# A two-layer hybrid decoder trunk on one core: one residue for the weight buffers, another order of the first loads, and small work moved off VectorE

## The chip, the cores and the metric

One core of one Trainium2 chip runs the whole program. The metric is the device time of one execution in microseconds. Three runs of the kernel before took 906.34, 906.39 and 908.03 us, median 906.39. Engines are named as the profile names them: PE is TensorE's matmul, PEld its weight load, DVE is VectorE, ACT is ScalarE, POOL is GpSimd, SP is SyncE, which issues most transfers.

## What is computed

Two layers act on x (256 tokens, 1,024 features, float32), conditioned by one vector c:

```python
c_act = silu(c)
for l in range(2):
    shift, scale, gate = split(c_act @ ada_w[l] + ada_b[l], 3)      # adaLN
    h = rmsnorm(x, norm_g[l]) * (1 + scale) + shift
    a_x, a_g, b_q, b_k, b_v, b_g, c_q, c_k, c_v, c_g, m_g = split(h @ w_in[l])
    ya = rg_lru(causal_conv4(a_x), ...) * silu(a_g)                 # softplus(lambda) sets the decay
    yb = merged_dilated_attention(rope(qknorm(b_q)), rope(qknorm(b_k)), b_v) * silu(b_g)
    yc = rmsnorm(gla(c_q, c_k, c_v, decay(h))) * silu(c_g)
    mg = sigmoid(m_g)                                               # three gates of 1024
    merged = mg[0]*(ya @ proj_a) + mg[1]*(yb @ proj_b) + mg[2]*(yc @ proj_c)
    x = x + gate * (merged @ w_o[l])
```

All of it is float32 to nearly full accuracy.

## The kernel before

**Products.** A float32 product is made of three fp32r matmuls: each operand is split into a rounded part `hi` and a rest `lo`, and hi·hi, hi·lo and lo·hi are summed in PSUM. x and h are kept with features on the partitions: eight tiles of 128 features x 256 tokens (`hhi`, `hlo`).

**Units.** The weights are streamed from HBM as 144 units a layer, each of 1,024 (or 768, 800) words a partition. A "T" unit (q, k, v, bg, c; two of the eight feature tiles) goes through `mm_t` (L777): h is stationary and the weights are the moving operand, 384, 400 or 512 columns; for bg the weights are stationary. An "F" or "P" unit (ax, ag, cq, ck, mA, mB, mC, pA, pB, pC, wo) goes through `mm_f` (L803): the weights are stationary, eight blocks of 128 x 128, and h, the merged input or a branch output (`yhi`, `ylo`) is the moving operand, 256 columns. Each step of a unit is three matmuls (L807 to L809, or L799 to L801). The first group of units of a layer is q, k, v, bg of head pair 0, four times: units 0 to 15.

**Buffers.** `load_next` (L191) issues a unit's transfer into one of six `raw` buffers. `advance` (L211) makes `hi` on ScalarE (L232) and `lo` on VectorE (L233) for the unit three ahead, in one of four `whi` and four `wlo` buffers; then the raw buffer is free and the next transfer is issued. `whi` and `wlo` are 1,040 words a partition, of which a unit takes the words from `o` on, `o` being 0 or 16 by the parity of its number and its kind (L224, L225).

**Where things lie.** Pools are laid out in the order in which they are opened, tiles in the order of their first use, each padded to 32 bytes a partition: `head` (vec_sb, c_sb, pos_sb, 896 bytes), `wts` (six raw, four whi, four wlo), `mov` (h), `one`, `two`, `sml`. By this the raw buffers start at a multiple of 256 bytes, and so do `wts` and `mov` as wholes; the four whi buffers are handed out in the order 0, 3, 2, 1. `yhi` starts 128 bytes past a multiple of 256.

**The start.** SP issues c, eye, x in two halves, vec, and then the items of `stream` (L84): four columns of adaLN (128 x 1024 each), units 0 to 3, four columns, units 4 to 7 and so on until 16 columns and units 0 to 15 are in. silu(c) is spread over the partitions (`crow`, L309 to L324) by eight small matmuls. `ada_tile` (L330) makes one column of shift or scale with a multiply-and-reduce on VectorE (L334), for a scale the product with norm_g (L336), and, once a pair is there, the tile of h (`h_tile`, L363): `tmp` = x · scale · rstd on VectorE (L366), `hi` on ScalarE (L368), `lo` on VectorE (L369). rstd comes from `stats_start` (L377), squares on ScalarE, three additions on VectorE, two matmuls with ones, and `rstd_full` (L346). The splits of units 0 to 3 are ordered behind rstd (`issue_after`, L230, L231).

**Small work.** `tables` (at unit 2) loads positions and makes the rope angles (`angles`, L419, VectorE but for two sines) and `rope_tables` (L441, eight VectorE products). `small` (at unit 16) makes softplus of lambda (`softplus`, L396, on VectorE but for one exponential) for the gates of branch A (`gen_a`, L502: sp4, sp4n, hb). The rest of the work of the branches is cut into generators that `pump` (L759) advances after each unit by a budget. A scheduler orders instructions on each engine's queue by priority and the `issue_after` marks.

```python
        if it in early:
            raw_t[n] = early[it]
            cur["sy", "a", it[2]] = SY.dma_start(out=early[it], in_=ada[it[1], it[2]]).ins
            return load_next()
```

Of the kernel before, what the change touches and what calls it, by code (L numbers as in the profile page):

```python
# [10 lines left out]
F32 = mybir.dt.float32  # L11
F32R = mybir.dt.float32r
# [114 lines left out]
def hybrid_trunk(ctx: ExitStack, tc: tile.TileContext, ws, ada, vec, gates, a2, qkg, c_t, x_t, pos, inv, eye,  # L127
# [13 lines left out]
    wts = ctx.enter_context(tc.tile_pool(name="wts", bufs=LEAD + 1))  # L141
    mov = ctx.enter_context(tc.tile_pool(name="mov", bufs=1))
# [165 lines left out]
    cact = sml.tile([P, KT], F32, name="cact")  # L308
    crow = one.tile([P, KT, P], F32, name="crow")  # L309
# [6 lines left out]
    V.tensor_scalar(b1, b1, 1.0, None, ALU.add)  # L316
    diag = one.tile([P, KT, P], F32, name="diag", tag="pt0")
    V.tensor_tensor(diag, eye_sb.unsqueeze(1).to_broadcast([P, KT, P]), cact.unsqueeze(2).to_broadcast([P, KT, P]), ALU.mult)
# [5 lines left out]
    crow2 = crow.rearrange("p k n -> p (k n)")  # L324

# [4 lines left out]
    def ada_tile(l, c, w):  # L330
# [61 lines left out]
    sp4 = sml.tile([P, L, KT], F32, name="sp4")  # L392
    sp4n = sml.tile([P, L, KT], F32, name="sp4n")
    hb = sml.tile([P, L, 2 * KT], F32, name="hb")

    def softplus():  # L396
        lam = vec_sb[:, :, V_LAM:V_LAM + KT]
        e, s, s2, p = (sml.tile([P, L, KT], F32, name=f"spl{i}") for i in range(4))
        V.scalar_tensor_tensor(e, lam, -1.0, lam, ALU.mult, ALU.max)
        A.activation(e, e, AF.Exp, scale=-1.0)  # L400
        V.tensor_scalar(s, e, 2.0, None, ALU.add)
        V.reciprocal(s, s)
        V.tensor_tensor(s, s, e, ALU.mult)
        V.tensor_tensor(s2, s, s, ALU.mult)
        V.tensor_scalar(p, s2, 1.0 / 17.0, None, ALU.mult)
        for k in range(7, 0, -1):
            V.scalar_tensor_tensor(p, p, 1.0 / (2 * k + 1), s2, ALU.add, ALU.mult)
        V.scalar_tensor_tensor(p, p, 1.0, s, ALU.add, ALU.mult)
        V.tensor_scalar(e, lam, -1.0, 0.0, ALU.mult, ALU.max)
        V.scalar_tensor_tensor(p, p, 2.0, e, ALU.mult, ALU.add)  # L410
        V.tensor_scalar(sp4, p, 0.5 * LRU_C, None, ALU.mult)
        V.tensor_scalar(sp4n, p, -0.5 * LRU_C, None, ALU.mult)
        V.tensor_scalar(hb, vec_sb[:, :, V_BA:V_BA + 2 * KT], 0.5, None, ALU.mult)
# [5 lines left out]
    def angles():  # L419
        pf = sml.tile([P, 2], F32, name="an0")  # L420
        an, k = (two.tile([P, 2, 32], F32, name="an", tag=t) for t in ("ra", "rb"))
        V.tensor_copy(pf, pos_sb)
        for t in range(2):
            V.tensor_scalar(an[:, t], inv_sb, pf[:, t:t + 1], None, ALU.mult)
        V.tensor_scalar(k, an, float(1.0 / (2 * np.pi)), 12582912.0, ALU.mult, ALU.add)
        V.tensor_scalar(k, k, -12582912.0, None, ALU.add)
        c1 = 6.28125
        c2 = float(np.float32(np.round((2 * np.pi - c1) * 2**21) / 2**21))
        c3 = float(2 * np.pi - c1 - c2)
        for c in (c1, c2, c3):  # L430
            V.scalar_tensor_tensor(an, k, -c, an, ALU.mult, ALU.add)
# [9 lines left out]
    def rope_tables(l):  # L441
# [5 lines left out]
        for i in range(2):  # L447
            g = gq[:, i].rearrange("p g (e d) -> p g e d", e=2)
            for t in range(2):
                V.tensor_tensor(ct[:, i, t].rearrange("p g (e d) -> p g e d", e=2), g,  # L450
                                cs[:, t].unsqueeze(1).unsqueeze(1).to_broadcast([P, 3, 2, 32]), ALU.mult)
                V.tensor_tensor(st[:, i, t].rearrange("p g (e d) -> p g e d", e=2), g,
                                sn[:, t].unsqueeze(1).to_broadcast([P, 3, 2, 32]), ALU.mult)
# [520 lines left out]
    def small():  # L974
# [3 lines left out]
        V.tensor_scalar(vec_sb[:, :, V_ON:V_ON + 2], vec_sb[:, :, V_ON:V_ON + 2], 0.5, None, ALU.mult)  # L978
# [102 lines left out]
```

## Time and profile before

| | |
|---|---|
| median of 3 runs | 906.39 us (906.34 to 908.03) |
| the profiled execution | 906.63 us, of which the span of instructions is 904.9 us |
| TensorE busy | 865.6 us, 96% of the span, 6,340 matmuls |
| VectorE busy | 671.9 us, 74% |
| ScalarE busy | 531.8 us, 59% |
| GpSimd busy | 179.1 us, 20% |
| HBM | 168 MB read, 187 GB/s over the span |
| granted TensorE clock | 0.987 of full, over the span |

A stretch's row gives the busy time of each engine with the number of instructions, the granted clock, the share of the 16 DMA engines that was in use and the rate. A timeline row gives the start, the duration, engine, line and operands of one instruction, and in brackets the idle time of its engine before it and what ended that. Matmuls are pipelined: how fast they follow each other is read from their starts.

### The profile page before, as it was taken

The numbers are of one execution on the slowest core, as the hardware profiler recorded it, in microseconds if no ns is written. First come the engines' busy times: TensorE is split into PE (matmuls) and PEld (weight loads), VectorE is DVE, ScalarE is ACT, GpSimd is POOL, SyncE is SP. The second block draws the span as 40 slices with busy tenths as digits, with TensorE's granted clock in tenths as the row PEclk, the third lists the DMA queues.
The fourth block names the chain that finished last, engine by engine and source line by source line (L and its number), as shares of the span: only waits on it lengthen the run. The fifth ranks groups of instructions, "written<-read, shape, count | busy, mean of one in ns | idle before, by whom it ended". The sixth has DMA issues, their size and how long they took to land.

```text
span 904.9 us, 16407 instructions
## 1 busy us (share of the span) xinstructions
PE 865.6 (96%) x6340; PEld 818.7 (90%) x6340; DVE 671.9 (74%) x1115; ACT 531.8 (59%) x897; POOL 179.1 (20%) x160
## 2 busy tenths in 40 slices
PE   3989999999999999999999999989999999999998
PEld 2978999999988888998989999979999988899998
DVE  6998899669667667656776788986896666656674
ACT  4376976686544554644454689666874545554451
POOL 0026365224000110100030525651430001000000
PEclk7999999999999999999999999999999999999999
DMA  8884456446756666676654644553567455455651
GB/s 334 309 290 138 146 174 193 141 134 195 248 184 197 205 212 201 212 236 205 224 168 148 191 146 144 176 194 117 184 205 239 163 189 166 148 173 187 191 167 47
DMA packets 52111, 170.16 MB, mean 188 GB/s; under 512 B 6240, under 2 KB 8160, under 8 KB 52032
## 3 DMA queue, kind: packets, MB, share of 16 engines
q1 hardware_dynamic: 51216, 167.04, 56.8%
q10 hardware_dynamic: 672, 1.87, 0.7%
q8 instruction: 50, 0.82, 0.4%
q0 software_dynamic: 144, 0.20, 0.2%
q14 instruction: 29, 0.24, 0.1%
HBM read 168.23 MB, written 1.05 MB: 187 GB/s over the span
## 4 chain that ended last, share of the span: by engine, by line
PE 51%; DVE 19%; DMA 12%; issue 8%; ACT 5%; POOL 4%; DVEq 0%; SPq 0%; ACTq 0%
DMA raw<-in_ada_dram 10%; PE mm L807 10%; PE mm L809 10%; PE mm L808 10%; DVE wlo L233 8%; PE mm L799 5%; PE mm L800 5%; PE mm L801 4%; POOL ss L570 2%; PE xps L177 1%; ACT whi L232 1%; DVE raw L334 1%; DVE rb L564 1%; DMA g_raw<-in_gates_dram 1%; DVE ra L562 1%
## 5 line engine op out<-in xcount | busy, mean ns | idle before, releaser
L233 DVE TENSOR_TENSOR wlo<-raw,whi 128x1024 fp32r<-128x1024 f32 (+2 forms) x288 | 335.3, 1171 | 84.5 <-ACT whi L232 83.1
L232 ACT CAST whi<-raw 128x1024 fp32r<-128x1024 f32 (+2 forms) x288 | 280.1, 976 | 185.2 <-PE mm L808 120.4
L807 PE MATMUL mm<-hhi,whi 128*128 128x256 f32 x768 | 217.1, 283 | 2.9 <-DVE rb L564 2.9
L809 PE MATMUL mm<-hhi,wlo 128*128 128x256 f32 x768 | 216.0, 282 | 3.5 <-DVE wlo L233 3.5
L808 PE MATMUL mm<-hlo,whi 128*128 128x256 f32 x768 | 215.4, 280 | 0.0
L799 PE MATMUL mm<-whi,hhi 128*128 128x384 f32 (+2 forms) x480 | 169.5, 358 | 7.2 <-ACT hhi L368 6.5
L800 PE MATMUL mm<-wlo,hhi 128*128 128x384 f32 (+2 forms) x480 | 171.3, 358 | 1.6 <-DVE wlo L233 1.4
L801 PE MATMUL mm<-whi,hlo 128*128 128x384 f32 (+2 forms) x480 | 167.6, 355 | 0.5 <-DVE hlo L369 0.5
L807 PEld LDWEIGHTS mm<-hhi,whi 128*128 128x128 f32 x768 | 146.0, 190 | 4.5 <-ACT tmp L857 2.9
L809 PEld LDWEIGHTS mm<-hhi,wlo 128*128 128x128 f32 x768 | 145.6, 190 | 4.7 <-DVE wlo L233 4.1
L808 PEld LDWEIGHTS mm<-hlo,whi 128*128 128x128 f32 x768 | 145.7, 190 | 0.3
L799 PEld LDWEIGHTS mm<-whi,hhi 128*128 128x128 f32 x480 | 92.9, 195 | 14.5 <-ACT hhi L368 7.5
L800 PEld LDWEIGHTS mm<-wlo,hhi 128*128 128x128 f32 x480 | 93.4, 195 | 9.1 <-DVE wlo L233 3.2
L334 DVE CUSTOM_DVE_ANT_0 raw<-raw,crow,vec_sb 128x1024 f32<-128x1024 f32 x38 | 48.7, 1283 | 70.2 <-DMA raw<-in_ada_dram 70.2
L801 PEld LDWEIGHTS mm<-whi,hlo 128*128 128x128 f32 x480 | 92.5, 194 | 6.7 <-DVE hlo L369 0.8
L807 PE MATMUL mm<-yhi,whi 128*128 128x256 f32 x320 | 89.9, 281 | 1.5 <-DVE mg L949 1.5
L808 PE MATMUL mm<-ylo,whi 128*128 128x256 f32 x320 | 89.4, 279 | 0.0
L809 PE MATMUL mm<-yhi,wlo 128*128 128x256 f32 x320 | 89.2, 279 | 0.0
L807 PEld LDWEIGHTS mm<-yhi,whi 128*128 128x128 f32 x320 | 60.4, 189 | 2.5 <-DVE mg L949 1.7
L809 PEld LDWEIGHTS mm<-yhi,wlo 128*128 128x128 f32 x320 | 60.1, 188 | 0.8 <-DVE mod L334 0.4
L808 PEld LDWEIGHTS mm<-ylo,whi 128*128 128x128 f32 x320 | 60.1, 188 | 0.0
L708 POOL TENSOR_TENSOR at_hl<-att_sb,at_hl 128x384 fp32r<-128x384 f32 x8 | 8.8, 1096 | 206.3 <-ACT at_hl L707 206.3
(236 smaller groups left out, 1409.2 us busy)
## 6 DMA issues: line engine op xcount, KB each, us to landing
raw<-in_ws_dram SPq DMA_DIRECT2D x192, 512.0 KB, 4.2
raw<-in_ws_dram SPq DMA_DIRECT2D x88, 384.0 KB, 3.1
raw<-in_ada_dram SPq DMA_DIRECT2D x38, 512.0 KB, 4.5
raw<-in_ws_dram SPq DMA_DIRECT2D x8, 400.0 KB, 4.6
g_raw<-in_gates_dram ACTq DMA_DIRECT2D x3, 512.0 KB, 4.5
x_sb<-in_x_t_dram SPq DMA_DIRECT2D x2, 512.0 KB, 6.6
ada_yhi<-in_ada_dram SPq DMA_DIRECT2D x2, 512.0 KB, 7.8
ada_ylo<-in_ada_dram SPq DMA_DIRECT2D x2, 512.0 KB, 9.0
```

What stands on the lines that cost most here:

```text
L177: seen[0] = T.transpose(*a, **k).ins
L232: A.copy(hi, r)
L233: V.tensor_tensor(lo, r, hi.bitcast(F32), ALU.subtract)
L334: V.tensor_tensor_reduce(w, w, crow2, 1.0, b, ALU.mult, ALU.add, a if i == 0 else m)
L562: V.tensor_tensor(ra.rearrange("p (g s) d -> p g s d", g=3), z4, ctab[l][:, i, t].unsqueeze(2).to_broadcast(bc), ALU.mult)
L570: G.tensor_tensor(ss, ss, mhalf[:, 0:12].rearrange("p (a b) -> p a b", a=2), ALU.pow)
L799: T.matmul(o, ah, wh, start=(k == 0), stop=False)
L800: T.matmul(o, ah, wl, start=False, stop=False)
L801: T.matmul(o, al, wh, start=False, stop=(k == KT - 1))
L807: T.matmul(ps[:, 0:S], hi[:, a:b], xh[:, k], start=(k == 0), stop=False)
L808: T.matmul(ps[:, 0:S], hi[:, a:b], xl[:, k], start=False, stop=False)
L809: T.matmul(ps[:, 0:S], lo[:, a:b], xh[:, k], start=False, stop=(k == nk - 1))
```

## The change

Buffers: `whi` and `wlo` become 1,024 words; `o` is 16 for q, k and v and 0 for all others. `sp4` and `hb` (64 and 128 bytes a partition) move from `sml` to `head`, in front of the weights; `sp4n` (64 bytes) gets a pool of its own, `gap`, between `wts` and `mov`.

Start: adaLN columns 0 and 1 are issued ahead of x, and vec is issued from ScalarE's queue. Matmuls without use (`warm_up`) are added: eight on `ones` before the silu, two on `diag`, three within `rstd_full`. The sum of squares takes eight matmuls and no additions. The tile of h is made otherwise: VectorE multiplies x by rstd, a few tiles at a time and without the scale (`x_scaled`); ScalarE makes scale · xr + shift (`f`), then `hi`; VectorE subtracts. The product with norm_g goes to ScalarE. The order marks of units 0 to 3 change: the rounded parts of units 1 to 3 come after the first rounded tile of h, the rests after the first scaled x. `tables` is no longer ordered behind VectorE's part of the last h.

Small work: softplus but for the reciprocal, and the angles but for one operation, go to GpSimd (a fused pair of operations becomes two there) and ScalarE; the rope tables take two products instead of eight.

```diff
+    gap = ctx.enter_context(tc.tile_pool(name="gap", bufs=1))
...
             cur["sy", "a", it[2]] = SY.dma_start(out=early[it], in_=ada[it[1], it[2]]).ins
+            if it[2] == 1:
+                for i in range(2):
+                    SY.dma_start(out=x_sb[:, 4 * i:4 * i + 4], in_=x_t[:, 4 * i:4 * i + 4])
...
-                streamed = units[it[1]][1][0] == "T" and units[it[1]][1][1] != "bg"
-                o = 16 * ((it[1] % 2 == 0) != streamed)
-                hi = wts.tile([P, D + 16], F32R, name="whi", tag="whi")[:, o:o + e]
-                lo = wts.tile([P, D + 16], F32R, name="wlo", tag="wlo")[:, o:o + e]
+                o = 16 * (units[it[1]][1][1] in ("q", "k", "v"))
+                hi = wts.tile([P, D], F32R, name="whi", tag="whi")[:, o:o + e]
+                lo = wts.tile([P, D], F32R, name="wlo", tag="wlo")[:, o:o + e]
                 with ExitStack() as st:
                     if it[1] < 4:
-                        st.enter_context(tc.issue_after(cur["ra"]))
-                        st.enter_context(tc.issue_after(cur["rv"]))
+                        st.enter_context(tc.issue_after(cur["h0a" if it[1] else "ra"]))
                     A.copy(hi, r)
+                with ExitStack() as st:
+                    if it[1] < 4:
+                        st.enter_context(tc.issue_after(cur["xr0"]))
                     V.tensor_tensor(lo, r, hi.bitcast(F32), ALU.subtract)
...
+    sp4 = head.tile([P, L, KT], F32, name="sp4")
+    hb = head.tile([P, L, 2 * KT], F32, name="hb")
+    sp4n = gap.tile([P, L, KT], F32, name="sp4n")
...
+    A.dma_start(out=vec_sb, in_=vec)
     SY.dma_start(out=eye_sb, in_=eye)
-    for i in range(2):
-        SY.dma_start(out=x_sb[:, 4 * i:4 * i + 4], in_=x_t[:, 4 * i:4 * i + 4])
-    SY.dma_start(out=vec_sb, in_=vec)
...
+    warm_up(ones, 8)
...
+    warm_up(diag[:, 0:2].rearrange("p k n -> p (k n)"), 2)
...
-            V.tensor_tensor(m, a, vcol(l, V_NG + j), ALU.mult)
+            A.activation(m, a, AF.Copy, scale=vcol(l, V_NG + j))
         if l == 0 and i == 1:
-            h_tile(0, j, cur["rstd"], cur["h"])
+            h_first(j, cur["xr"], cur["h"])
...
+    def x_scaled(i, a, b):
+        if a == 0:
+            cur["xr"][i] = one.tile([P, 4, S], F32, name="xr", tag=("pt1", "pt0")[i])
+        v = V.tensor_tensor(cur["xr"][i][:, a:b], x_sb[:, 4 * i + a:4 * i + b],
+                            cur["rstd"].unsqueeze(1).to_broadcast([P, b - a, S]), ALU.mult)
+        cur.setdefault("xr0", v.ins)
+
+    def h_first(j, xr, h):
+        if j in (1, 2, 4):
+            x_scaled(j // 4, j % 4, 2 if j == 1 else 4)
+        hi, lo, f = h[0], h[1], tmp()
+        A.activation(f, xr[j // 4][:, j % 4], AF.Identity, bias=mod[:, 0, 1, j:j + 1], scale=mod[:, 0, 0, j:j + 1])
+        a = A.copy(hi[:, j], f)
+        cur.setdefault("h0a", a.ins)
+        v = V.tensor_tensor(lo[:, j], f, hi[:, j].bitcast(F32), ALU.subtract)
+        cur["h_last"] = (a.ins, v.ins)
...
-            if i % 2:
-                V.tensor_tensor(sq[i - 1], sq[i - 1], t, ALU.add)
-        V.tensor_tensor(sq[0], sq[0], sq[2], ALU.add)
         ps = xps()
-        for j in range(2):
-            T.matmul(ps[:, 0:S], ones, sq[0][:, j], start=(j == 0), stop=(j == 1))
+        for j in range(KT):
+            T.matmul(ps[:, 0:S], ones, sq[j // 2][:, j % 2], start=(j == 0), stop=(j == KT - 1))
...
-        for k in range(7, 0, -1):
-            V.scalar_tensor_tensor(p, p, 1.0 / (2 * k + 1), s2, ALU.add, ALU.mult)
+        for k in range(6, -1, -1):
+            G.tensor_tensor(p, p, s2, ALU.mult)
+            G.tensor_scalar(p, p, 1.0 / (2 * k + 1), None, ALU.add)
...
         for c in (c1, c2, c3):
-            V.scalar_tensor_tensor(an, k, -c, an, ALU.mult, ALU.add)
+            G.tensor_scalar(kc, k, -c, None, ALU.mult)
+            G.tensor_tensor(an, an, kc, ALU.add)
...
-    rstd = rstd_full(sts)
+    rstd = rstd_full(sts, 3)
+    cur["rstd"], cur["xr"] = rstd, {}
+    x_scaled(0, 0, 1)
...
         a, v = cur["h_last"]
-        with tc.issue_after(a), tc.issue_after(v):
+        with tc.issue_after(a):
```

## Rows read from the trace of the kernel before

**Rows 1.** Busy time by stretch, whole program: us, busy us (x instructions) by engine

```profile
20.00:40.00 20.00, 19.66 (x115) 19.65 (x116) 20.00 (x39) 8.23 (x12) 0.00 (x0) 0.88 0.88 327
40.00:60.00 20.00, 18.67 (x115) 16.92 (x114) 19.79 (x45) 10.51 (x16) 2.89 (x1) 1.00 0.93 331
60.00:80.00 20.00, 15.79 (x116) 14.98 (x115) 19.88 (x44) 14.11 (x30) 13.38 (x13) 0.91 0.45 151
80.00:905.00 825.00, 805.95 (x5982) 762.67 (x5980) 599.96 (x960) 490.58 (x827) 161.45 (x141) 1.00 0.56 179
```

**Rows 2.** Transfers by line: size and median us from issue to landing

```profile
x_sb<-in_x_t_dram SPq DMA_DIRECT2D x2, 512.0 KB, 6.6
...
ada_yhi<-in_ada_dram SPq DMA_DIRECT2D x2, 512.0 KB, 7.8
```

**Rows 3.** Timeline of the start: start us, duration us, instruction

```profile
7.95 2.27 ACT L381 ACTIVATE sq<-x_sb 128x512 f32<-128x512 f32 x4 [5.32 <-DMA x_sb<-in_x_t_dram]
...
11.82 2.05 PE L388 MATMUL xps<-sq,ones 128*128 128x256 f32 x4 [3.76 <-DVE sq L385]
...
18.02 0.42 DVE L357 SCALAR_TENSOR_TENSOR rs_y<-rs_q,rs_y 128x256 f32<-128x256 f32 x1
18.36 0.98 DVE L233 TENSOR_TENSOR wlo<-raw,whi 128x800 fp32r<-128x800 f32 x1
...
20.34 0.70 PE L799 MATMUL mm<-whi,hhi 128*128 128x400 f32 x1 [6.47 <-ACT hhi L368]
```

**Rows 4.** Timeline of TensorE, four F units one behind the other

```profile
164.32 0.28 PE L808 MATMUL mm<-hlo,whi 128*128 128x256 f32 x1
...
169.74 0.28 PE L809 MATMUL mm<-hhi,wlo 128*128 128x256 f32 x1
...
175.18 0.28 PE L809 MATMUL mm<-hhi,wlo 128*128 128x256 f32 x1
```

**Rows 5.** Timeline of TensorE, T units of 384 columns

```profile
119.45 0.34 PE L801 MATMUL mm<-whi,hlo 128*128 128x384 f32 x1
...
121.19 0.34 PE L799 MATMUL mm<-whi,hhi 128*128 128x384 f32 x1
...
124.70 0.34 PE L801 MATMUL mm<-whi,hlo 128*128 128x384 f32 x1
```

**Rows 6.** Groups of VectorE and ScalarE by line: busy us, mean ns

```profile
L366 DVE SCALAR_TENSOR_TENSOR tmp<-x_sb,mod,rs_y 128x256 f32<-128x256 f32 x8 | 3.7, 479 | 0.0
L384 DVE TENSOR_TENSOR sq<-sq 128x512 f32<-128x512 f32 x2 | 1.4, 692 | 4.9 <-ACT sq L381 4.9
L336 DVE TENSOR_TENSOR mod<-acc,vec_sb 128x1 f32<-128x1 f32 x8 | 1.2, 153 | 0.0
L431 DVE SCALAR_TENSOR_TENSOR an<-an 128x64 f32<-128x64 f32 x3 | 0.7, 218 | 0.0
...
L407 DVE SCALAR_TENSOR_TENSOR spl<-spl,spl 128x16 f32<-128x16 f32 x7 | 2.0, 284 | 0.0
...
L368 ACT ACTIVATE hhi<-tmp,mod 128x256 fp32r<-128x256 f32 x8 | 4.0, 509 | 10.1 <-DVE tmp L366 10.1
```

**Rows 7.** Timeline of VectorE and GpSimd, small operations

```profile
60.93 0.18 DVE L407 SCALAR_TENSOR_TENSOR spl<-spl,spl 128x16 f32<-128x16 f32 x1
...
62.73 1.66 POOL L568 TENSOR_TENSOR ro<-ra,rb 128x192 f32<-128x192 f32 x1
...
63.87 0.56 DVE L407 SCALAR_TENSOR_TENSOR spl<-spl,spl 128x16 f32<-128x16 f32 x1
...
71.70 0.20 POOL L569 TENSOR_SCALAR ss<-ss 128x12 f32<-128x12 f32 x1
```

**Rows 8.** Busy time by stretch: the granted clock is the third number from the end

```profile
20.30:24.40 4.10, 4.06 (x13) 4.05 (x14) 4.10 (x7) 1.32 (x2) 0.00 (x0) 0.50 1.02 412
...
65.00:70.00 5.00, 2.31 (x18) 2.15 (x17) 5.00 (x11) 3.35 (x9) 1.27 (x3) 0.90 0.86 278
70.00:75.00 5.00, 5.00 (x36) 4.99 (x35) 5.00 (x13) 1.98 (x4) 4.83 (x5) 0.76 0.50 163
```

More of the change, by code (lines that the diff above doesn't have):

```diff
@@ L315, in hybrid_trunk @@
     b1 = vec_sb[:, :, V_ADA:V_ADA + 16].rearrange("p l (j i) -> p l j i", i=2)[:, :, :, 0]
-    V.tensor_scalar(b1, b1, 1.0, None, ALU.add)
     diag = one.tile([P, KT, P], F32, name="diag", tag="pt0")
-    V.tensor_tensor(diag, eye_sb.unsqueeze(1).to_broadcast([P, KT, P]), cact.unsqueeze(2).to_broadcast([P, KT, P]), ALU.mult)
+    v = V.tensor_tensor(diag, eye_sb.unsqueeze(1).to_broadcast([P, KT, P]), cact.unsqueeze(2).to_broadcast([P, KT, P]), ALU.mult)
+    with tc.issue_after(v.ins):
+        V.tensor_scalar(b1, b1, 1.0, None, ALU.add)
     for e in range(2):
@@ L382, in stats_start @@
             sq.append(t)
-            if i % 2:
-                V.tensor_tensor(sq[i - 1], sq[i - 1], t, ALU.add)
-        V.tensor_tensor(sq[0], sq[0], sq[2], ALU.add)
         ps = xps()
-        for j in range(2):
-            T.matmul(ps[:, 0:S], ones, sq[0][:, j], start=(j == 0), stop=(j == 1))
-        return ps
-    sp4 = sml.tile([P, L, KT], F32, name="sp4")
-    sp4n = sml.tile([P, L, KT], F32, name="sp4n")
-    hb = sml.tile([P, L, 2 * KT], F32, name="hb")
+        for j in range(KT):
+            T.matmul(ps[:, 0:S], ones, sq[j // 2][:, j % 2], start=(j == 0), stop=(j == KT - 1))
+        return ps
     def softplus():
@@ L398, in softplus @@
         e, s, s2, p = (sml.tile([P, L, KT], F32, name=f"spl{i}") for i in range(4))
-        V.scalar_tensor_tensor(e, lam, -1.0, lam, ALU.mult, ALU.max)
+        A.activation(e, lam, AF.Abs)
         A.activation(e, e, AF.Exp, scale=-1.0)
-        V.tensor_scalar(s, e, 2.0, None, ALU.add)
+        G.tensor_scalar(s, e, 2.0, None, ALU.add)
         V.reciprocal(s, s)
-        V.tensor_tensor(s, s, e, ALU.mult)
-        V.tensor_tensor(s2, s, s, ALU.mult)
-        V.tensor_scalar(p, s2, 1.0 / 17.0, None, ALU.mult)
-        for k in range(7, 0, -1):
-            V.scalar_tensor_tensor(p, p, 1.0 / (2 * k + 1), s2, ALU.add, ALU.mult)
[L408 to L413, printed above, removed]
+        G.tensor_tensor(s, s, e, ALU.mult)
+        G.tensor_tensor(s2, s, s, ALU.mult)
+        G.tensor_scalar(p, s2, 1.0 / 17.0, 1.0 / 15.0, ALU.mult, ALU.add)
+        for k in range(6, -1, -1):
+            G.tensor_tensor(p, p, s2, ALU.mult)
+            G.tensor_scalar(p, p, 1.0 / (2 * k + 1), None, ALU.add)
+        G.tensor_tensor(p, p, s, ALU.mult)
+        A.activation(e, lam, AF.Relu, scale=-1.0)
+        G.tensor_scalar(p, p, 2.0, None, ALU.mult)
+        G.tensor_tensor(p, p, e, ALU.add)
+        G.tensor_scalar(sp4, p, 0.5 * LRU_C, None, ALU.mult)
+        G.tensor_scalar(sp4n, p, -0.5 * LRU_C, None, ALU.mult)
+        G.tensor_scalar(hb, vec_sb[:, :, V_BA:V_BA + 2 * KT], 0.5, None, ALU.mult)
     cs = one.tile([P, 2, 32], F32, name="cs")
@@ L419, in angles @@
     def angles():
-        pf = sml.tile([P, 2], F32, name="an0")
-        an, k = (two.tile([P, 2, 32], F32, name="an", tag=t) for t in ("ra", "rb"))
-        V.tensor_copy(pf, pos_sb)
+        pf, an, k = ((sml if i == 0 else one).tile([P, 2] if i == 0 else [P, 2, 32], F32, name=f"an{i}") for i in range(3))
+        G.tensor_copy(pf, pos_sb)
         for t in range(2):
-            V.tensor_scalar(an[:, t], inv_sb, pf[:, t:t + 1], None, ALU.mult)
-        V.tensor_scalar(k, an, float(1.0 / (2 * np.pi)), 12582912.0, ALU.mult, ALU.add)
-        V.tensor_scalar(k, k, -12582912.0, None, ALU.add)
+            G.tensor_scalar(an[:, t], inv_sb, pf[:, t:t + 1], None, ALU.mult)
+        G.tensor_scalar(k, an, float(1.0 / (2 * np.pi)), 12582912.0, ALU.mult, ALU.add)
+        G.tensor_scalar(k, k, -12582912.0, None, ALU.add)
         c1 = 6.28125
@@ L429, in angles @@
         c3 = float(2 * np.pi - c1 - c2)
+        kc = two.tile([P, 2, 32], F32, name="an", tag="ro")
         for c in (c1, c2, c3):
-            V.scalar_tensor_tensor(an, k, -c, an, ALU.mult, ALU.add)
+            G.tensor_scalar(kc, k, -c, None, ALU.mult)
+            G.tensor_tensor(an, an, kc, ALU.add)
         lim = 3.1415925
@@ L434, in angles @@
         A.activation(sn[:, :, 0, :], an, AF.Sin)
-        V.scalar_tensor_tensor(k, an, -1.0, an, ALU.mult, ALU.max)
+        A.activation(k, an, AF.Abs)
         A.activation(cs, k, AF.Sin, bias=hpi, scale=-1.0)
-        V.tensor_scalar(sn[:, :, 1, :], sn[:, :, 0, :], -1.0, None, ALU.mult)
+        G.tensor_scalar(sn[:, :, 1, :], sn[:, :, 0, :], -1.0, None, ALU.mult)
     ctab, stab = {}, {}
@@ L447, in rope_tables @@
         for i in range(2):
[L448 to L453, printed above, removed]
+            g = gq[:, i].rearrange("p g (e d) -> p (g e) d", e=2)
+            V.tensor_tensor(ct[:, i].rearrange("p t g (e d) -> p t (g e) d", e=2),
+                            g.unsqueeze(1).to_broadcast([P, 2, 6, 32]),
+                            cs.unsqueeze(2).to_broadcast([P, 2, 6, 32]), ALU.mult)
+            V.tensor_tensor(st[:, i], gq[:, i].unsqueeze(1).to_broadcast([P, 2, 3, 64]),
+                            sn.rearrange("p t e d -> p t (e d)").unsqueeze(2).to_broadcast([P, 2, 3, 64]), ALU.mult)
         ctab[l], stab[l] = ct, st
@@ L961, in hybrid_trunk @@
     sts = stats_start()
-    rstd = rstd_full(sts)
+    rstd = rstd_full(sts, 3)
+    cur["rstd"], cur["xr"] = rstd, {}
+    x_scaled(0, 0, 1)
     h = h_alloc(0)
     hhi["h"] = h
-    cur["rstd"], cur["h"] = rstd, h
+    cur["h"] = h
     def tables():
         a, v = cur["h_last"]
-        with tc.issue_after(a), tc.issue_after(v):
+        with tc.issue_after(a):
             load_after(("sy", "a", 3), (pos_sb, pos), (inv_sb, inv.partition_broadcast(P)))
@@ L977, in small @@
             softplus()
-        V.tensor_scalar(vec_sb[:, :, V_ON:V_ON + 2], vec_sb[:, :, V_ON:V_ON + 2], 0.5, None, ALU.mult)
+        G.tensor_scalar(vec_sb[:, :, V_ON:V_ON + 2], vec_sb[:, :, V_ON:V_ON + 2], 0.5, None, ALU.mult)
     sts = layer(0, h, {2: tables, 15: load_small, 16: small})
```

## The prediction

> **What bounds the kernel now.** I read the busy time by stretch first [rows 1]. From 80 us to the end TensorE is busy in 806 of 825 us: there the time is the number of matmuls times their spacing, and the other engines have room. From 20 to 80 us VectorE is the full engine, 59.7 of 60 us, while TensorE sits idle for 5.9 us and runs partly at half speed. Before 20 us the work waits for the first transfers [rows 2, 3]. So the change has two separate effects: the spacing of matmuls over the whole span, and VectorE's work in the first 80 us.
>
> For the start, the transfers and the timeline: x lands 6.6 us after its issue and the first adaLN column 7.8 us after [rows 2]; the squares start at 7.95, the sum on TensorE ends near 13.9, rstd is ready near 18.4, and the first projection starts at 20.34 [rows 3]. For the spacing, TensorE's timeline: start to start, not durations.
>
> **Addresses.** In the kernel before, the four whi (and wlo) buffers are 4,160 bytes apart, so their starts step by 64 bytes modulo 256, and the offset of 16 words puts F units (weights stationary, h moving) at 64 or 192 and q, k, v units at 0 or 128. h starts at 0. By the pool sizes worked out by hand, the new head pool is 192 bytes longer: all buffers at 192, q, k, v at 192+64 = 0, h again at 0.
>
> F matmuls of 256 columns show two spacings: 46 steps from 164.32 to 169.74 are 117.8 ns each, in two units at 192; the 48 steps from there to 175.18 are 113.3 ns, in the next two units, at 64, with no break between [rows 4]. The spacing stays what it is until something disturbs it. I counted restarts after a break over the whole timeline: on a unit at 192, 26 of 27 settled in the slow spacing; on one at 64, 20 of 35 in the fast one. Eight times a slow stretch turned fast exactly where 192 passed to 64. About half of the F matmuls run at each, mean 115.55 ns. With 192 alone the way back to fast is gone.
> - F units that read h or the merged input: 56 a layer (ax, ag, cq, ck, the three m, wo), 24 matmuls each, 2 layers: 2,688. I take four in five slow, 116.9 ns: 1.35 x 2,688 = **+3.6 us**. Ends: all slow +6.0, all fast -6.0.
> - q, k, v: 48 units a layer with 12 matmuls, 1,152 in all. At 0, 10 steps from 119.45 to 121.19 are 174.0 ns; at 128, the 20 steps from there to 124.70 are 175.5 [rows 5]. Half of them, 576, gain 1.5 ns: **-0.9 us**.
> - c units: 384 matmuls whose moving weights now lie at 192, which no row shows. The 4.5 ns between the F spacings bounds them at -1.7 and +1.7; I take **0**, since the moving rows nearest to it differ by only 1.5 ns.
> - F units that read the branch outputs (at 128): 960 matmuls. Both spacings occur there at both residues: **0**, ends -2.2 and +2.2.
>
> Addresses together: +2.7 us, from -10.8 to +9.0.
>
> **VectorE up to 80 us.** One operation holds the next up by its duration less some 0.08 us (L357 takes 0.42 from 18.02, the next starts at 18.36 [rows 3]). The durations are those of [rows 6], where nothing else is named.
> - The scaled x: eight of 0.48 go, 8 x 0.40 = -3.2; in their place 2,048 columns by rstd, at 0.61 for 512 (L384's 0.69) = +2.4. Net -0.8. The subtraction becomes a plain one: 0.42, as L357 of the same size, for the 0.48 of the scaled kind: -0.5.
> - Eight products for mod go to ScalarE: 8 x 0.07 = -0.6.
> - Angles: ten of about 0.2 (L431) leave, -1.2. The tables' columns stay the same in fewer operations: 0.
> - Softplus: 18 leave; seven L407 are 2.0 us, eleven of some 0.18 (a free L407, [rows 7]) are 2.0, less 18 x 0.08: -2.6.
> - Two scalings on vec leave or move into VectorE's idle time before 8 us: -0.2.
>
> Sum -5.9 us. ScalarE takes eight passes more like L368's 0.51 us, and the small products: it is busy 8.2 and 10.5 us of 20 from 20 to 60 [rows 1], which covers them; were it full, about 4 us would show.
>
> 37 small operations arrive on GpSimd instead. What they cost VectorE shows in [rows 7]: L407 at 63.87 took 0.56 us while GpSimd's L568 was under way, against 0.18 for its like at 60.93. A small GpSimd operation with nothing beside it took 0.20 us. Ends: 0 and 37 x 0.20 = 7.4 us. Softplus is needed late (sp4 by the gates), so many of its 24 can run after 80 us, where VectorE has room: I take **+2.0**.
> The Trainium skill (SBUF — State Buffer, "SBUF: two separate sides") says a VectorE operation with two SBUF inputs and a GpSimd one that reads SBUF hold a shared port pair in turn, for a whole instruction; the row agrees, and by that rule the term would be near its upper end.
>
> **Order of the start.** Columns 0 and 1 go ahead of x on SP's queue; at the 412 GB/s of the transfers near 20 us [rows 8] 512 KB take 1.3 us, so x is some 2.6 us later, near 10.5 us, and column 0 takes x's place, near 8. vec moves to ScalarE's queue, where the table load waits behind one more issue, beside the wait for c. The three additions of squares go; TensorE sums eight tiles in place of two, each two records of 0.51 us at the half clock [rows 3], 8.2 us if it stays there, half of that otherwise, beside the squares' 2.3 us. The sum then ends between 13.8 and 19.3; I take 16.3, against 13.9. But the two columns that stood among rstd's operations are done by then, and its five operations of some 0.42 need 2.6 us with their hand-overs: rstd comes near 18.9, against 18.4, with the same work behind it done: **0**, ends -2 and +3. The warm-up matmuls stand in TensorE's idle time. The lo parts of units 0 to 3 now wait for the first scaled x, which VectorE itself makes; what queues behind them are columns that have not landed yet.
>
> **Clock.** The first 4.1 us of projections ran at 0.50 and 70 to 75 us at 0.76, after 2.7 us of idle time [rows 8]. The 1.2 GHz stretch could give back 2.0 us, but VectorE is the bound behind it: -0.5; less idle time before 70 us: -0.8. **-1.3**, ends 0 and -3.2.
>
> Start together: -5.9 + 2.0 + 0 - 1.3 = -5.2 us, from -11 to +4.5. It reaches the end in full, since TensorE's idle and half-speed time up to 80 us is about 9 us and nothing after gives slack back.
>
> **Sum.** -5.2 + 2.7 = -2.5. The profiled execution took 906.63 us (span 904.9, 1.7 around it): 904.1. The median of the runs is 0.24 lower: **903.9 us**. A measurement of this kernel can tell about 0.2%, 1.8 us, from no change.
>
> **Rivals.**
> 1. *GpSimd gives VectorE nothing* (slower). Place: VectorE's operations from 34 to 80 us. If each of the 37 operations holds them for 0.20 us, the start gives 5.2 - 5.4, nothing, and the addresses' +2.7 remains: 906.4 + 2.9 = 909.3. It decides from 0.17 us each. For: the 0.56 us row, and VectorE without a pause there. Against: part of the 37 may run late. Chance 0.22.
> 2. *One residue keeps all fast.* If nothing flips the spacing once all weights lie alike, F and branch units run at 113.3: -6.0 - 2.2 - 0.9, with the start -14.3: 892.1. For: fast stretches do last across units at 192. Against: 26 of 27 restarts. Chance 0.15.
> 3. *Addresses do nothing*, or the buffers don't lie where I reckon; the mixture stays and only the start counts: 901.2. For: restarts at 64 go both ways. Chance 0.20. The Trainium skill (the same page and section) says TensorE's reads of SBUF wait on nobody, the shared pair being the only contention among engines, which would give this case; the two spacings at full clock are not explained by it.
>
> The forecast itself has 0.43, its own range 900 to 908.
>
> **Numbers.** 893 to 910 leaves out half of rival 2, the upper part of rival 1 and little else. Faster: 0.24 of the forecast, 0.15, 0.18 of rival 3, so 0.57. Slower: 0.06 of the forecast and 0.17 of rival 1, 0.23. The rest, 0.20, is the same.
>
> **What would show it.** F units at 117.8 ns almost everywhere (rival 2: 113.3; rival 3: both). q, k, v at 174.3. VectorE's last split of the first group some 3 us earlier than now; no softplus on it. GpSimd busy between 34 and 80 us, and L233 longer beside it if rival 1 holds. The first projection near 20 us and at the full clock. I am wrong if the stretch after 80 us gets shorter, or if the first group ends no earlier.

## The result, and the profile after

The changed kernel is slower: 918.12 us median of 4 runs (915.85 to 920.45) against 907.21 of the kernel before (906.34 to 911.06), ratio 1.0125, 95% interval 1.0098 to 1.0152. That is 11 us more, where 2.5 us less was forecast. The profiled execution took 917.97 us, span 916.2; it is compared below with the 904.9 of the kernel before.

I numbered the 5,376 matmuls of the units in their order on TensorE and took the difference of the start of each n-th one between the two traces. It tells where the time went: 0.00 us for the first, -1.5 at 30 us, +4.4 for the 140th (45 us before, 49 after), back to -1.2 for the 280th (73 us), +7.6 for the 340th (81 and 88 us), +6.3 for the 420th, +11.8 for the 2,220th (408 us), +7.7 for the 2,370th, +11.3 at the end. So there are two jumps before 90 us, then a slow growth, with one step back near 420 us. Of the growth 2.6 us come between the 540th and the 860th matmul (60.2 us in the kernel before, from 118 us on, and 62.8 in the changed one); the experiments come back to this third loss.

Busy time by stretch, the changed kernel (us, busy us and instructions of PE, PEld, DVE, ACT, POOL, clock, DMA share, GB/s):

```profile
20.00:40.00 20.00, 19.12 (x116) 17.69 (x117) 18.48 (x29) 12.05 (x23) 10.55 (x12) 1.00 0.89 324
40.00:60.00 20.00, 16.47 (x90) 15.09 (x89) 17.47 (x28) 11.52 (x19) 0.59 (x1) 0.91 0.84 275
60.00:80.00 20.00, 14.85 (x113) 14.01 (x111) 13.81 (x22) 13.37 (x30) 17.27 (x32) 0.98 0.65 228
80.00:916.00 836.00, 816.62 (x6006) 772.04 (x6006) 605.00 (x955) 494.16 (x839) 165.85 (x146) 0.99 0.55 176
45.00:50.00 5.00, 5.00 (x21) 4.97 (x20) 5.00 (x8) 2.25 (x4) 0.00 (x0) 0.66 0.79 246
80.00:85.00 5.00, 2.75 (x13) 2.78 (x14) 5.00 (x9) 0.41 (x1) 4.27 (x6) 0.50 0.00 0
```

Against [rows 1], VectorE is no longer the full engine: 49.8 of 60 us instead of 59.7. Yet TensorE gets less done: 90 matmuls instead of 115 from 40 to 60 us. The engine that fills is GpSimd, 17.3 of 20 us from 60 to 80. An engine that has work and is idle waits for somebody; the waits show for whom.

The first jump, timeline of GpSimd, VectorE, ScalarE and TensorE near 40 us (start, us, instruction, idle time before it and what ended it):

```profile
32.56 1.06 POOL L445 TENSOR_SCALAR an<-an 128x64 f32<-128x64 f32 x1
...
35.89 1.28 ACT L456 ACT_TABLE_LOAD   x1
...
38.62 0.32 POOL L453 TENSOR_TENSOR an<-an,an 128x64 f32<-128x64 f32 x1
...
38.97 0.20 DVE L455 TENSOR_SCALAR an<-an 128x64 f32<-128x64 f32 x1 [1.52 <-POOL an L453]
...
39.20 0.26 ACT L456 ACTIVATE sn<-an 128x64 f32<-128x64 f32 x1 [2.03 <-DVE an L455]
...
41.87 0.54 DVE L474 TENSOR_TENSOR stab<-gq,sn 128x384 f32<-128x384 f32 x1
...
43.74 1.85 DVE L236 TENSOR_TENSOR wlo<-raw,whi 128x800 fp32r<-128x800 f32 x2
...
44.77 0.46 PE L822 MATMUL mm<-wlo,hhi 128*128 128x400 f32 x1 [2.44 <-DVE wlo L236]
```

The angles are one chain of dependent small operations. On GpSimd it runs from 28.0 to 38.9 us. Operations of 64 columns took up to 1.25 us there while VectorE was busy (1.06 at 32.56), and 0.32 to 0.37 us while it was idle (0.32 at 38.62). On VectorE the one operation that stayed there (L455) stands in the queue for 1.52 us until the chain is done; on ScalarE the sine stands for 2.03 us. What is queued behind them are the splits of the next units: VectorE then still makes the tables (1.9 us from 41.87) before the split that TensorE waits for, at 43.74. The Trainium skill (PSUM — Partial Sum Buffer, "Engine vs sequencer instructions") says that the queues of ScalarE, VectorE and GpSimd are strictly first in, first out; the rows agree.

The second jump, the same engines near 80 us:

```profile
62.28 0.22 POOL L422 TENSOR_TENSOR spl<-spl,spl 128x16 f32<-128x16 f32 x1
...
74.66 0.25 POOL L433 TENSOR_SCALAR sp4n<-spl 128x16 f32<-128x16 f32 x1
74.98 0.60 POOL L589 TENSOR_TENSOR ro<-ra,rb 128x192 f32<-128x192 f32 x1
75.54 1.58 POOL L590 TENSOR_TENSOR ro<-ra,rb 128x192 f32<-128x192 f32 x1
...
77.49 2.31 POOL L592 TENSOR_TENSOR ss<-ss,mhalf 128x12 f32<-128x12 f32 x1
...
79.83 1.34 DVE L597 TENSOR_TENSOR ro<-ro,ss 128x768 f32<-128x768 f32 x1 [3.17 <-POOL ss L592]
...
82.25 0.55 PE L829 MATMUL mm<-hhi,whi 128*128 128x256 f32 x1 [4.95 <-DVE rb L586]
```

Softplus occupies GpSimd's queue from 62 to 75 us, and the rope sums and the power for q and k (L589 to L592) come between and behind. `ss` is ready at 79.8; in the kernel before the same power ended at 74.3 and VectorE had its product with `ss` (L575) at 74.42:

```profile
71.98 2.30 POOL L570 TENSOR_TENSOR ss<-ss,mhalf 128x12 f32<-128x12 f32 x1
...
74.42 1.26 DVE L575 TENSOR_TENSOR ro<-ro,ss 128x768 f32<-128x768 f32 x1
```

In the changed kernel VectorE waits 3.17 us for it (the fence above), behind that product stand the two that empty the PSUM bank of k (L584, L586), and TensorE waits 4.95 us for that bank. Around this pause the granted clock falls to half (0.50 over 80 to 85 us above), as it was 0.66 over 45 to 50 us behind the first jump.

The spacing, timeline of TensorE with 72 steps in F units that read h:

```profile
175.51 0.28 PE L830 MATMUL mm<-hlo,whi 128*128 128x256 f32 x1
...
178.34 0.28 PE L830 MATMUL mm<-hlo,whi 128*128 128x256 f32 x1
...
181.16 0.28 PE L830 MATMUL mm<-hlo,whi 128*128 128x256 f32 x1
...
183.99 0.28 PE L830 MATMUL mm<-hlo,whi 128*128 128x256 f32 x1
```

They are 117.8 ns each on average, in all three units; the mixture of [rows 4] is gone here. I took every step from start to start after 100 us and sorted them by the residues of the weights and of the moving operand. Means in ns:

| | before | after | matmuls | difference, us |
|---|---|---|---|---|
| F units that read h | 115.54 | 117.60 | 2,688 | +5.5 |
| F units that read branch outputs | 115.67 | 116.54 | 960 | +0.8 |
| bg | 114.46 | 117.79 | 192 | +0.6 |
| q, k, v | 174.56 | 173.56 | 1,152 | -1.2 |
| c | 230.42 | 233.28 | 384 | +1.1 |

Together +6.8 us, an estimate that takes these means for all matmuls of a kind. The step back near 420 us is a pause and the clock behind it: the kernel before waits 1.8 us for a split (L233) at 420.5 us and runs at half speed until 424.0, the changed kernel does neither there. The kernel before has one more such stretch of 3.4 us near 472, the changed kernel two, near 301 and 479, each behind pauses. Single runs of one kernel scatter by some 4 us to either side. The clock is a small part of that: in the 23 runs of the kernel before in the first series (903.72 to 911.43 us) the mean granted clock goes from 0.985 to 0.998, and its correlation with the time is -0.28; what makes the rest stays open. That is why each experiment is read twice: as a median, and by the stretch of its trace that it is about.

### The profile page after: what moved, and what is told of

It reads as the page before. It is cut to its first block, busy times and chain, and to the rows that moved or that the text cites. A ratio compares the mean times of both kernels' runs of the same rounds, so it can differ in the third digit from the quotient of the medians.

```text
span 916.2 us, 16507 instructions
## 1 busy us (share of the span) xinstructions
PE 880.5 (96%) x6378; PEld 829.8 (91%) x6378; DVE 665.2 (73%) x1055; ACT 539.2 (59%) x924; POOL 196.1 (21%) x197
## 4 chain that ended last, share of the span: by engine, by line
PE 59%; DMA 13%; DVE 12%; issue 6%; ACT 5%; POOL 5%; SPq 0%; DVEq 0%; ACTq 0%; POOLq 0%
PE mm L829 11%; PE mm L831 11%; PE mm L830 11%; DMA raw<-in_ada_dram 9%; PE mm L822 6%; PE mm L823 6%; PE mm L821 6%; DVE wlo L236 6%; ACT whi L232 2%; PE xps L178 2%; POOL ss L592 2%; DMA ada_hraw<-in_ada_dram 1%; PE ps_s L174 1%; PE xps L174 1%; DMA pos_sb<-in_pos_dram 1%
```

## Experiments

**Addresses alone, and their opposite.** The first takes the addresses of the changed kernel into the kernel before (the hunks on `gap`, `o`, `whi`, `wlo`, `sp4`, `hb`, `sp4n`), the second takes them out of the changed kernel (and moves the two angle tiles, for room).

> The kernel before, with nothing but the changed kernel's addresses. Theory A (two losses: the addresses, and a start that GpSimd's small operations hold up): F units that read h all at about 117.6 ns in place of a mean of 115.5, branch units at 116.5 in place of 115.7, q/k/v 1.1 ns and c 2.9 ns apart from before, bg 117.8 for 114.5; over the span +6 to +7.5 us, so 913 to 915. Rival B (addresses are nothing, all of the loss is the start): 907. Rival C (addresses are all of it): 917 to 919.

> The changed kernel with the addresses of the kernel before (the two angle tiles moved for room to where the kernel before had them). Theory A: F units again a mixture with a mean near 115.5 ns, the stalls of the start unchanged (TensorE idle for 2.4 us near 42 us and 5 us near 77 us): 910.5 to 912.5. Rival B: 917 to 919. Rival C: 906 to 908.

Measured: 912.13 us, ratio 1.0047 (1.0022 to 1.0072), +4.9 us; and 913.59, 1.0070 (1.0047 to 1.0094), 4.5 us less than the changed kernel. Spacing of F units that read h: 117.49 in the first; in the second a mixture again, 114.9 at 64 and 116.0 at 192. The two jumps before 90 us stand unchanged in the second trace (+5.0 for the 140th matmul, +7.6 for the 340th) and are absent from the first. Theory A, though each time lies about 1 us outside the range that it gave; B and C both fall, since their times lie outside the intervals.

**GpSimd's work put back on VectorE**, softplus alone and then the angles too (the functions of the kernel before in place of the new ones).

> The changed kernel with softplus as it was, on VectorE. Theory A: GpSimd's row of rope sums and power no longer stands behind 20 operations, ss is ready some 5 us earlier, VectorE does not wait 3.2 us for it and TensorE not 5.0 us near 77 us, nor runs at half speed behind it; the stall near 42 us stays: 911 to 914. Rival B (any small GpSimd operation slows VectorE by the port, and softplus's own work on VectorE costs the same): within 2 us of 918. Rival C (addresses are all of it): 918.

> The changed kernel with softplus and the angles both back on VectorE; addresses, order of loads, warm-up, the new tile of h and the two-product tables stay. Theory A: both stalls go, the rest of the start is worth 2 to 5 us, the addresses' +6.9 stays: 908 to 911. Rival C: 918. Rival D (the stall near 42 us comes from the tables that are ordered ahead of the splits, not from GpSimd): no better than the run with softplus alone put back.

Measured: 914.14 us, 1.0074 (1.0048 to 1.0100), and 912.94, 1.0064 (1.0048 to 1.0081). By the trace the first is +3.2 us against the kernel before at the 340th matmul instead of +7.6, with the jump at 42 us still there (+4.5 for the 140th); the second is -2.0 and -1.8 at these places, so both jumps are gone. In the medians softplus is worth 4.0 us; the angles show 1.2 us there, within the scatter, though 5 us in the trace at 80 us. Of these 5 us, 1.6 are not the angles' doing: the second run is that much ahead at the 70th matmul already, since its sum of squares ran at the full clock (last section). The times alone settle less than the traces: rival B stands at the edge of the first interval, the second median lies above the 908 to 911 expected, and rival D is not told from theory A by the two medians. By the traces D falls, since the jump at 42 us went while the tables stayed where they were.

**All three undone**: addresses, softplus and angles. What is left is the order of the first loads, the warm-up, the sum of squares, the new tile of h and the two-product tables.

> The changed kernel with softplus and angles on VectorE and the addresses of the kernel before: what is left are the order of the first loads, the warm-up, the sum of squares without additions, the new tile of h and the two-product tables. Theory A: the run with both back less the addresses' 5 us: 906 to 908, the start 2 to 3 us ahead at 120 us and the F mixture of the kernel before. Rival B (the loss is all in the start): 912 to 914.

Measured: 906.99 us against 908.95 for the kernel before in the same series, 0.9985 (0.9962 to 1.0008): no difference that can be told. The 420th matmul comes 2.9 us earlier, but the 860th no longer does: from the 540th to the 860th it takes 63.0 us against 60.2. All runs above that have the changed kernel's order of work show this loss (62.8 to 64.3 us), with either addresses and with or without GpSimd; the one with the addresses alone does not (60.5). In ratios to the kernel before, the addresses cost 1.0064 - 0.9985, 0.79%, and the move to GpSimd 1.0070 - 0.9985, 0.85%. With the -0.15% of the rest that is 1.49%, against 1.25% measured (0.98 to 1.52). So in net the two causes make the whole loss, about half each, and each known to some 0.3% only. What is left is a gain at the start and a loss behind it that cancel. From the other side they come out smaller: 0.47% for the addresses in the kernel before, 1.0125 - 1.0070 = 0.55% in the changed one, and 1.0125 - 1.0064 = 0.61% for the move.

**Is it GpSimd or the queue?** Softplus is back on VectorE. The angles stay on GpSimd, but what waits for them on VectorE and ScalarE is queued behind the split of unit 13:

```diff
+    def tables2():
+        with tc.issue_after(cur["lo", 13]):
+            sines(*cur["an"])
+            rope_tables(0, cur["gq"])
...
-    sts = layer(0, h, {2: tables, 15: load_small, 16: small})
+    sts = layer(0, h, {2: tables, 12: tables2, 15: load_small, 16: small})
```

> The changed kernel with softplus back on VectorE and the angles left on GpSimd, but the operations that wait for them on VectorE and ScalarE (the clip, the sines, the tables) queued behind VectorE's split of unit 13, near 54 us, where the kernel before had them. Theory H (the loss near 42 us is queue order: VectorE and ScalarE stand in order behind a chain that GpSimd has not finished): no wait for GpSimd before 50 us, no stall of TensorE near 42 us, the first group ends 4 to 6 us earlier than with softplus alone put back, the time is that of the run with both put back or less: 909.5 to 913. Rival I (GpSimd's operations themselves slow VectorE through the port, wherever they stand): VectorE's splits beside them are longer by 0.2 us each and the first group ends no more than 2 us earlier: 913 to 916.

Measured: 904.97 us, 0.9974 (0.9953 to 0.9995), although all weights still lie at 192: better than either theory said, and 8 us better than with the angles back on VectorE. From the run with softplus alone put back (1.0074) it differs by this queueing only, and is 9 us faster; by the trace 4.6 us at the 140th matmul, 5.4 at the 340th and 10.6 at the 860th. Its timeline:

```profile
29.61 3.34 POOL L442 TENSOR_SCALAR an<-inv_sb,an 128x32 f32<-128x32 f32 x2
33.03 1.07 POOL L443 TENSOR_SCALAR an<-an 128x64 f32<-128x64 f32 x1
...
35.51 2.12 DVE L236 TENSOR_TENSOR wlo<-raw,whi 128x768 fp32r<-128x768 f32 x2
...
40.92 0.81 POOL L451 TENSOR_TENSOR an<-an,an 128x64 f32<-128x64 f32 x1
...
53.38 0.18 DVE L456 TENSOR_SCALAR an<-an 128x64 f32<-128x64 f32 x1
```

The chain on GpSimd is even longer, to 41.7 us, and nobody waits for it: L456 follows at once at 53.38. VectorE pays a little for it, 2.12 us for two splits of 768 that take 0.95 each alone. So the same operations on the same engine cost 5 us or next to nothing, by where their consumer stands in its queue. Theory H; the port of rival I is real, but small. The 8 us over the run with both put back come later: at the 420th matmul the two are level (-2.7 and -3.0 us against the kernel before), at the 860th they are 4.3 us apart. From the 540th to the 860th this run takes 59.6 us: the third loss is gone. It goes with the early tables, since the operations of the later units are queued in another order, too. A wait of TensorE between 118 and 184 us (in all, times, longest) in the run with both put back, then in this one:

```profile
PE mm L819 <- DVE wlo L236: 1.7, 2, 1.0
```

```profile
PE mm L826 <- DVE wlo L236: 0.7, 1, 0.7
```

Which operation in that order makes the difference, and where the rest of the 8 us lies, no run shows.

**Other residues**, in the kernel before: all weights at 0, 64 or 128, q, k and v at 0 (by `o` and the place of sp4, hb, sp4n).

> The kernel before with all weight buffers at a multiple of 256 bytes, q, k, v too (buffers of 1,024 words, no offset); h stays at a multiple of 256, the branch outputs 128 past it. Theory A (the spacing of an F unit goes by where the weights lie against the moving operand, each residue with its own): F units that read h all near one value, not the mixture of 115.5 ns; 0 has not been seen, so 113.3 (then about -7 us, 900) or 117.8 (+6, 913). Rival E (any single residue loses the way back to the fast spacing, whatever it is): 117.5 here and at 64 and 128 alike. q, k, v 173.6; c at 227 to 229.

> The kernel before with all weight buffers 64 bytes past a multiple of 256, q, k, v at a multiple of 256; h as before. Theory A: two thirds or more of the F units fast (67% of them were at 64 beside others at 192), mean 113.5 to 114.5 ns, so -2.5 to -5.5 us: 901 to 905. Rival E: 117.5, 913.

> The kernel before with all weight buffers 128 bytes past a multiple of 256, q, k, v at a multiple of 256; h as before. Theory A: one value of its own, unseen; as q, k, v lose 1.5 ns with the moving operand at 128, I lean to the slow spacing for h and to the fast one for the branch outputs, which then lie alike with the weights: 908 to 914. Rival E: 117.5, 913.

Measured, one execution each: 914.23, 910.53 and 913.07 us, against 908.95. The run at 64 missed its 901 to 905: that forecast counted the units that read h, while the branch units, then 192 apart, lost (117.59 instead of 115.67 ns). At 0 the spacing is neither of the two values named. The spacing says more than these single times. Timelines of TensorE, 24 steps of an F unit that reads h, with the weights at 0 (first fence) and at 128 (second):

```profile
171.73 0.28 PE L808 MATMUL mm<-hhi,wlo 128*128 128x256 f32 x1
...
174.61 0.28 PE L808 MATMUL mm<-hhi,wlo 128*128 128x256 f32 x1
```

```profile
171.80 0.28 PE L808 MATMUL mm<-hlo,whi 128*128 128x256 f32 x1
...
174.65 0.28 PE L808 MATMUL mm<-hlo,whi 128*128 128x256 f32 x1
```

These are 120.0 and 118.8 ns a step. The means over the span, sorted by residues:

| weights minus moving operand, modulo 256 | h at 0, weights there | branch output at 128 |
|---|---|---|
| 0 | 119.77 (weights at 0) | 119.80 (weights at 128) |
| 64 | 114.65 (at 64) | 116.54 (at 192, the changed kernel) |
| 128 | 118.68 (at 128) | 118.68 (at 0) |
| 192 | 117.60 (at 192, the changed kernel) | 117.59 (at 64) |

At 0, 128 and 192 what counts is the distance between the two operands, not the place of either: the two columns agree within 0.03 ns. At 64 they do not, 114.65 against 116.54; why, no run shows. At 0 nearly every step is 120 ns, at 192 it is 118, at 128 the steps go through 115 to 122 in a repeating row; at 64 they are 113 or 118 for long stretches, and 71% of those that read h are fast, against 28% of the branch steps in the changed kernel. I had leaned to fast branch units at 128: wrong, equal residues are the slowest. Rival E falls too. The Trainium skill (TensorE: Matmul & The Clock Gate, "Step-by-step: what each phase is for") says that weights load through a read port of their own and take nothing from the running matmul; here the same matmul took 113.3 to 120.0 ns by where the weights lie against the moving operand, so the measurement does not bear that out. What in the chip makes the difference, no run shows.

**All F units 64 apart**: weights at 64, and the branch outputs moved to 0 in the kernel before.

```diff
-    inv_sb = one.tile([P, 32], F32, name="inv_sb")
...
+    inv_sb = one.tile([P, 32], F32, name="inv_sb")
     for c, t in enumerate(tiles):
```

> The kernel before with the weights at 64, q, k, v at 0, h at 0 and the branch outputs moved from 128 to 0 (inv_sb takes its place behind them). Theory F (the spacing of an F unit goes by the distance from the moving operand's start to the weights' start, modulo 256: 64 gives 114.65 to 116.5 ns, 192 gives 117.6, 128 gives 118.7, 0 gives 119.8): all F units lie 64 apart, about 70% fast, mean 114.7 for h and for the branches; 3,648 x 0.9 = -3.3 us, q, k, v -1.1: the time is 4 to 5 us under the kernel before. Theory G (it goes by the weights' own residue, or by the branch outputs' own): the branch units stay at 117.6, as in the run with 64 alone, and the time is within 2 us of the kernel before.

Measured: all F units 114.10 ns on average, 84% of the steps fast, better than expected: theory F. But the time is 906.23 against 907.24 us, 0.9984 (0.9962 to 1.0007), where 4 to 5 us had been expected. The waits of TensorE from 20 to 900 us (in all, times, longest) show where the gain went in the traces; in the first fence this kernel, in the second the kernel before:

```profile
PE xps L178 <- ACT pr L612: 4.3, 3, 2.1
...
PE mm L807 <- DVE mg L949: 2.9, 1, 2.9
```

```profile
PE xps L177 <- ACT pr L612: 2.3, 4, 1.0
PE mm L807 <- DVE mg L949: 1.5, 1, 1.5
```

And busy time in three stretches (the clock is third from the end), in the same order:

```profile
250.00:255.00 5.00, 4.91 (x30) 4.71 (x29) 3.02 (x5) 2.99 (x5) 0.00 (x0) 0.66 0.62 202
440.00:445.00 5.00, 3.81 (x22) 3.81 (x23) 5.00 (x12) 1.71 (x4) 0.00 (x0) 0.74 0.90 302
695.00:700.00 5.00, 5.00 (x31) 5.00 (x32) 2.98 (x5) 3.10 (x5) 0.00 (x0) 0.66 0.71 206
```

```profile
250.00:255.00 5.00, 4.92 (x38) 4.21 (x38) 3.38 (x5) 3.67 (x6) 0.00 (x0) 1.00 0.66 210
440.00:445.00 5.00, 4.81 (x42) 4.81 (x43) 5.00 (x12) 2.72 (x5) 0.00 (x0) 1.00 0.94 295
695.00:700.00 5.00, 5.00 (x43) 4.14 (x44) 4.51 (x7) 1.53 (x2) 0.00 (x0) 1.00 0.74 217
```

A faster TensorE comes sooner to work that ScalarE and VectorE have not finished. The waits for the softmax (L612) grow from 2.3 to 4.3 us, that for the merge (L949) from 1.5 to 2.9, and behind each of these pauses the clock is at half speed for some 3.4 us, in three places against the two of the kernel before (near 421 and 472 us, outside these stretches). By the means the spacing is worth some 6.8 us here (an estimate); TensorE's idle time from 20 to 900 us grows by 5.5 us, from 27.6 to 33.1, and one more stretch at half speed costs 1.7. So in that one execution all of the gain turned into waits. That the other nine runs lost it the same way is not shown.

**Putting it together.** The changed kernel with the addresses just tried, the tables late, and softplus and the angles on GpSimd at the very beginning; then the same with the two small transfers for the angles back where the changed kernel has them, and the angles behind them.

```diff
-    A.dma_start(out=pos_sb, in_=pos)
...
-    G.dma_start(out=inv_sb, in_=inv.partition_broadcast(P))
...
+            load_after(("sy", "a", 3), (pos_sb, pos), (inv_sb, inv.partition_broadcast(P)))
```

> The changed kernel's start, with softplus and the angles on GpSimd but done at the very beginning (behind the first small transfers, softplus first, then the angles; everything before 20 us, where GpSimd and VectorE have nothing else to do), the clip, the sines and the tables behind VectorE's split of unit 13, the weights at 64, q, k, v, h and the branch outputs at 0. Theories F and H together: no stall near 42 or 77 us, at 100 us some 4 to 6 us ahead of the kernel before (the run with both put back was 2 to 3 ahead and still had softplus on VectorE), F units at 114.7: 897 to 902. If the early GpSimd operations hold the first columns on VectorE up (rival I), the first matmul comes after 20 us and 902 to 905 is left.

> The run with all lessons, but positions and inv loaded where the changed kernel loads them, behind the first columns, and the angles on GpSimd after that; softplus stays at the very beginning. There the first columns landed 1.4 us and x 2.8 us later than in the changed kernel, and the first projection began at 23.6 us. If the 288 small packets of these two transfers held up the large ones: x lands near 10 us, the first projection begins at 18.5 to 20.8 us, and the time falls by 2 to 4 us, to 898 to 901. If it was GpSimd's early softplus (its operations took up to 1.15 us beside VectorE's columns), the start stays as late as it was and the time within 1 us of 902.5.

Measured: 902.55 us, 0.9949 (0.9920 to 0.9978), and 900.66, 0.9918 (0.9893 to 0.9943). The second beats both kernels, the one before by 6.7 us. Transfers by line (KB each, median us to landing), in the first fence with the early small transfers, in the second without:

```profile
ada_yhi<-in_ada_dram SPq DMA_DIRECT2D x2, 512.0 KB, 7.6
x_sb<-in_x_t_dram SPq DMA_DIRECT2D x2, 512.0 KB, 10.2
```

```profile
ada_yhi<-in_ada_dram SPq DMA_DIRECT2D x2, 512.0 KB, 6.2
x_sb<-in_x_t_dram SPq DMA_DIRECT2D x2, 512.0 KB, 8.2
```

Without them x lands 2 us sooner and the first projection begins at 20.77 instead of 23.55. Softplus is just as early in both, and the angles of the first begin at 14.19 us only, when x had landed (13.57): the small transfers it was, though not which of the two. The medians alone would not tell, their intervals overlap. From 20 to 80 us the second kernel works on 362 matmuls, the changed one on 314, the one before on 341.

## Why the prediction was wrong, point by point

- **VectorE's work, -5.9 us.** It did go: up to the 420th matmul VectorE is busy 73.0 us instead of 81.0, a part of that being branch work that came later. But the step "It reaches the end in full" failed. VectorE was the bound because every operation of its queue was ready; I counted what left the queue and not that two operations stayed in it which now wait for another engine, 1.52 and 3.17 us. I asked what is queued behind a wait only of the order marks of units 0 to 3, not of these two. The price itself was near: with the tables late and softplus back, where -3.3 of the -5.9 apply, the 420th matmul comes 2.7 us earlier, behind a first projection 0.5 us later. The reason given, "nothing after gives slack back", failed as well: the run with all three undone was 2.9 us ahead at 93 us and level at 178.
- **GpSimd, +2.0 (0 to 7.4).** The step that failed: "Softplus is needed late (sp4 by the gates), so many of its 24 can run after 80 us". They were not late, they stood in front: 22 of them between 62 and 75 us, ahead of the power that q and k need. I priced what they take from VectorE and not what they do to their own queue. The row that I read for the port (0.56 us) is real, but the cost falls mostly on the other side: splits of 1,024 on VectorE took 1.21 to 1.51 us up to 84 us, against 1.21 to 1.46 before, while GpSimd's operations of 64 columns took up to 1.25 instead of 0.32 to 0.37. The 0.20 us "with nothing beside it" was misread: VectorE's L858 ran beside it, from 71.48 to 72.21 us. The Trainium skill's rule (SBUF — State Buffer, "SBUF: two separate sides") speaks of a lock that either side can wait on; the rows agree, but here it is mostly GpSimd that waits. Rival 1 had the right sign and engine with the wrong mechanism; its 909.3 took the addresses' +2.7 with it.
- **Start, 0, and the clock, -1.3.** x landed at the time I took, and the first projection began at 20.34 in both: right, though the half clock during the sum of squares had a part in it; in the two runs without it the first projection began at 18.5. The clock gained before 40 us (1.00 instead of 0.88) and lost it behind the two pauses, which I had not foreseen.
- **Addresses, +2.7.** Direction and mechanism were right, the size was not. "Four in five slow" was 96%: 117.60 ns, not 116.9, and +5.5 us instead of +3.6. The branch units, put at 0, cost 0.8; c, put at 0 because "the moving rows nearest to it differ by only 1.5 ns", cost 1.1, inside its bounds; bg, 0.6, I left out. q, k, v came as forecast. The sum is 6.8 us by the steps and between 4.5 and 7.2 by the three pairs of runs. Rivals 2 and 3 both fell: one residue does set one spacing for the units that read h, but at this distance the slow one.

So the forecast had the addresses too small by 2 to 4.5 us, and the start wrong in sign: -5.2 foreseen, +6.3 by the 420th matmul.

## What to carry to other kernels

Work that moves to an idle engine is priced by three queues: the new engine's, where it stands in front of somebody, the consumer's, where everything behind the consumer now waits as well, and only then the old one's. Moved work can stay where it was moved to if its consumer is queued late: the same angles on GpSimd cost 5 us or next to nothing. A faster matmul is worth its full gain only where the engines that feed TensorE have room.

## What had not been expected of the hardware

- The spacing of a matmul with 256 moving columns depends on the distance of the starts of its two operands modulo 256 bytes: 119.8 ns at 0, 118.7 at 128, 117.6 at 192, 113 or 118 at 64, in shares that differ from run to run.
- Operations of 64 columns on GpSimd took 0.32 to 0.37 us while VectorE was idle and up to 1.25 while it was busy.
- Two transfers of 17 KB in all, early among the first ones, put x off by 2.0 us.
- The sum of squares (eight matmuls, two records each) took 3.72 us in the two runs with both put back, 5.41 in the changed kernel and 6.05 in the first run that puts all together. From 12 to 14 us the granted clock is 1.00 in the first two and 0.50 in the others, whose TensorE had been idle for longer before. The run with softplus and the angles back, then the one that took longest:

```profile
10.48 3.72 PE L410 MATMUL xps<-sq,ones 128*128 128x256 f32 x16 [1.88 <-ACT sq L406]
```

```profile
13.23 6.05 PE L412 MATMUL xps<-sq,ones 128*128 128x256 f32 x16 [5.14 <-ACT sq L408]
```
